# Hybrid decoder trunk, MLP stage: four additional matmuls behind the norm's mean, weights and operand from one tile, into a bank pair of the down products

## The chip, the core and the metric

One core of one Trainium2 chip runs the whole program. The metric is the time of one execution in device microseconds, as the median of several runs. Lower is better.

## The reference, cut to what matters

Four layers run one after the other over 512 tokens of width 1024: a latent attention mixer, an MLP, a gated linear attention mixer and a second MLP. All of it is in float32. The change touches both MLPs.

```
def rms_norm(x, gain):
    y = x * lax.rsqrt(jnp.mean(x * x, axis=-1, keepdims=True) + EPS)
    return y * gain

def sq_relu_mlp(xn, w_up, w_down):          # w_up 1024 x 4096, w_down 4096 x 1024
    hid = jnp.square(jax.nn.relu(xn @ w_up))
    return hid @ w_down
...
x = x + sq_relu_mlp(rms_norm(x, norm_mlp[i]), mlp_w_up[i], mlp_w_down[i])
return rms_norm(x, final_norm)
```

## The kernel before

**Precision.** A float32 matrix is held as two parts of type float32r, high and low (`split`, L110). The high part is a rounded copy written by ScalarE (ACT, L112), the low part is the remainder, written by VectorE (DVE, L115). A product is three matmuls on TensorE (PE): high by high, high by low, low by high. Each matmul instruction has a load of a 128x128 weight block of its own (a row of PEld) and a stream of the moving operand (a row of PE).

**The MLP.** Its two matrix products are written as block products with sums of blocks, so that fewer matmuls are needed. The up part works on 8 column blocks of `w_up` (`up_block`, L846), each with 7 products; the down part (`down_block`, L987) joins two of them and has 7 products too, woven between the up products. Each product runs through `matmuls` (L824), whose line L826 issues all of them: 128x128 weights and a moving operand of 256 columns. An up product is 24 of them, a down product 48. The weights are the split tiles `wh` and `wl` (three buffers each). The moving operands are the split input tiles `x0h` to `x7l`, their sums `T0h` to `T3l`, and for the down products the tile `h`. One product at the start of each MLP, that of block 1, takes its weights from a pair of tiles called `w`, which lie where `T3h` and `T3l` are put later (L907).

**Placement.** The author sets tile positions by hand with unused pieces (`PADS`, L91), and the first `h` tile of each down block begins 40 elements earlier in its buffer than the later ones (L1002 to L1004). In the built program, in bytes of a partition, `x0h` lies at 151136, the first `wh` at 34720, `w` at 214624, and the first `h` at 109248 with its `wh` at 42912.

**The place of the change.** `mlp` (L809) opens its banks (a pool with one bank for `seed`, three for `u`, two pairs for `d`). Its first two matmuls (L1163) have both weights and moving operand from `x0h` and write a `seed` bank; nothing reads that result. Then come the first products of blocks 0 and 1 (24 matmuls with `wh` and `wl`, 24 with `w`), and then the mean of the squares for the norm (L255 in `mean`, one float32 matmul of 512 columns that the trace shows as two rows). The products that follow need the mean only when their results are scaled (L890). Instruction order on an engine comes from a scheduling layer; `keep_in_program_order` (called `kept` here) holds single instructions where the code has them. Fifteen up products follow the mean before the first down product, whose banks (`d`, L1013) are free until then.

Of the kernel before, what the change touches and what calls it, by code (L numbers as in the profile page):

```python
# [10 lines left out]
F32 = mybir.dt.float32  # L11
# [7 lines left out]
P = 128  # L19
# [6 lines left out]
TH = S // 2  # L26
# [23 lines left out]
def trunk_kernel(ctx: ExitStack, tc: tile.TileContext, t_in: dict, out: bass.AP, out_row: bass.AP):  # L50
    nc = tc.nc
    PE, ACT, DVE, POOL, SP = nc.tensor, nc.scalar, nc.vector, nc.gpsimd, nc.sync
# [6 lines left out]
    def opened(name, side="left", space=None):  # L59
        es = ExitStack()  # L60
        kw = {"space": space} if space is not None else {"side": side}
        now[name] = es, es.enter_context(tc.tile_pool(name=uname(name), bufs=1, reuse_waits="tile", **kw))
        return now[name][1]
# [9 lines left out]
    def uname(s):  # L73
        count[0] += 1
        return f"{s}_{count[0]}"
# [34 lines left out]
    def split(src, hi, lo, hi_eng=ACT, lo_eng=DVE, order=lambda i: i):  # L110
        if hi_eng is ACT:
            raised.append(order(ACT.activation(hi, src, AF.Copy)))  # L112
        else:
            hi_eng.tensor_copy(hi, src)
        return lo_eng.tensor_tensor(lo, src, f(hi), ALU.subtract)  # L115
# [29 lines left out]
    def piece(raw, a, n, order=lambda i: i):  # L145
        hi = sb.tile([P, a, n], F32R, tag="wh", bufs=3, name=uname("wh"))
        lo = sb.tile([P, a, n], F32R, tag="wl", bufs=3, name=uname("wl"))
        cut_at.append(split(raw, hi, lo, order=order))
        return hi, lo
# [659 lines left out]
    def mlp(layer, nrm, nxt, final=False):  # L809
# [342 lines left out]
        mp = opened("mps", space=bass.MemoryType.PSUM)  # L1152
# [4 lines left out]
        for n, (m0, tk) in {2: (0, first), 3: (0, second), 4: (KH, first), 5: (KH, second)}.items():  # L1157
            acc[n] = xall[:, m0 : m0 + KH, tk]

        t = mp.tile([P, 512], F32, tag="seed", name=uname("ps"))  # L1160
        for h in range(2):
            x = quad["11"][0][0]
            PE.matmul(t[:, h * TH : (h + 1) * TH], x[:, :P], x, start=h == 0, stop=True, skip_group_check=True)  # L1163
        for b in range(2):
            wide[b] = halves(wide_raw())
        for b, t in enumerate(halves(wide_raw())):
            fills[b](t)
        kept = tc.keep_in_program_order
        for b in range(2):
            blocks[b].pop(0)()  # L1170
        t = nrm.combine(KH - 1, dp.tile([P, 4, TH], F32, tag="q", bufs=6, name=uname("q")))
        kept(nrm.mean())
        made[1]["21"] = piece(made[1]["a12"], KH, 256)
        kept(cut_at[-1])
        kept(nrm.combined(KH - 1, t))
# [466 lines left out]
    n_mix1 = Mixer(ND, inv_d, "mix", ND, "A")  # L1642
    n_mlp0 = mlp_norm(0)
    mlp0 = mlp(0, n_mlp0, n_mix1)
    out_proj(t_in["mla_w_o"][0], O, n_mlp0, mlp0, begun)
    next(mlp0, None)
# [5 lines left out]
    class Final:  # L1652
# [39 lines left out]
        def row(self, t, c, p):  # L1692
# [19 lines left out]
            for eng, q, cs in ((ACT, ACT, slice(0, 384)), (DVE, SP, slice(384, D))):  # L1712
# [4 lines left out]
                q.dma_start(o[:, cs], y[:, cs])  # L1717

    mlp1 = mlp(1, n_mlp1, Final(), True)
    out_proj(t_in["gla_w_o"][0], Y, n_mlp1, mlp1)  # L1720
    next(mlp1, None)
# [53 lines left out]
```

## Time and profile before

| | us |
|---|---|
| median of 3 runs | 1066.1 |
| lowest and highest of them | 1065.54, 1068.97 |
| the profiled execution's own time | 1065.53 |
| its span, first to last instruction | 1063.8 |
| PE busy in it | 1055.4 |
| PEld busy | 975.8 |
| DVE busy | 856.6 |
| ACT busy | 642.4 |

A start or a window is in microseconds from the start of the span. Matmuls overlap: a row of PE lasts longer than the distance to the next one, so the pace is read from the starts, or from the chain of waits, where each piece counts once and has its number of instructions.

### The profile page before, as it was taken

To read this page: it belongs to the slowest core of one execution; us is meant where nothing else is said; L and a number is where in the kernel's file an instruction comes from. 1 tells how busy PE (TensorE), PEld (TensorE's weight loads), DVE (VectorE), ACT (ScalarE), POOL (GpSimd) and SP (SyncE) were. 2 spreads that over 40 slices of the span, in tenths; PEclk is the share of its full clock that TensorE was granted. 3 is DMA by queue.
4 is the path that set the end of the run, shared out by engine and by line. 5 is a ranking of instruction groups with operands and counts; after the bars stand their busy time and mean duration, and the time that the engine had idled before them with its cause. 6 is when DMAs were issued, how large, how long until landed. Compare 5 with 4: busy or idle time off the path is not lost.

```text
span 1063.8 us, 17962 instructions
## 1 busy us (share of the span) xinstructions
PE 1055.4 (99%) x7332; PEld 975.8 (92%) x7332; DVE 856.6 (81%) x1186; ACT 642.4 (60%) x937; POOL 78.8 (7%) x104
## 2 busy tenths in 40 slices
PE   9999999999999999999999999999999999999997
PEld 7788988999999999988788888888999999999986
DVE  6789879899799789967565654678999799799965
ACT  6577645575667777644334734655665667776734
POOL 7400001000000000030000000001000000000000
PEclk9999999999999999999999999999999999999999
DMA  7312017765553663360222211238665555654412
GB/s 219 91 50 80 7 34 217 165 193 145 173 141 118 179 155 112 99 203 26 53 77 80 80 59 61 80 99 218 179 141 154 158 126 159 173 127 117 139 40 79
DMA packets 114946, 127.81 MB, mean 120 GB/s; under 512 B 8640, under 2 KB 86736, under 8 KB 114864
## 3 DMA queue, kind: packets, MB, share of 16 engines
q1 hardware_dynamic: 98832, 108.15, 32.0%
q0 software_dynamic: 13792, 16.80, 10.2%
q10 hardware_dynamic: 2240, 1.73, 0.5%
q8 instruction: 57, 0.93, 0.4%
q14 instruction: 25, 0.20, 0.1%
HBM read 124.56 MB, written 2.10 MB: 119 GB/s over the span
## 4 chain that ended last, share of the span: by engine, by line
PE 96%; DVE 2%; ACT 0%; DMA 0%; issue 0%; ACTq 0%; DVEq 0%
PE ps L826 51%; PE ps L120 13%; PE ps L122 13%; PE ps L121 13%; PE ps L1426 2%; PE ps L137 1%; PE ps L1465 0%; PE ps L1432 0%; PE ps L1412 0%; PE ps L685 0%; PE ps L686 0%; PE ps L684 0%; PE ps L682 0%; PE ps L683 0%; DVE stat L695 0%; DMA gains<-in_gains_dram 0%
## 5 line engine op out<-in xcount | busy, mean ns | idle before, releaser
L112 ACT ACTIVATE wh<-raw 128x1024 fp32r<-128x1024 f32 x208 | 219.8, 1060 | 152.7 <-PE ps L826 99.4
L115 DVE TENSOR_TENSOR wl<-raw,wh 128x1024 fp32r<-128x1024 f32 x208 | 251.8, 1220 | 25.4 <-ACT wh L112 25.1
L826 PE MATMUL ps<-h,wh 128*128 128x256 f32 x1344 | 168.6, 278 | 0.0
L826 PEld LDWEIGHTS ps<-h,wh 128*128 128x128 f32 x1344 | 161.2, 188 | 0.0
L120 PE MATMUL ps<-set,wh 128*128 128x512 f32 x232 | 91.3, 394 | 0.0
L826 PE MATMUL ps<-h,wl 128*128 128x256 f32 x672 | 91.2, 278 | 0.0
L121 PE MATMUL ps<-set,wh 128*128 128x512 f32 x232 | 90.7, 391 | 0.1
L122 PE MATMUL ps<-set,wl 128*128 128x512 f32 x232 | 90.7, 391 | 0.0
L112 ACT ACTIVATE wh<-wraw 128x1024 fp32r<-128x1024 f32 x41 | 43.1, 1057 | 74.2 <-PE ps L122 41.5
L826 PEld LDWEIGHTS ps<-h,wl 128*128 128x128 f32 x672 | 83.6, 188 | 0.0
L879 POOL DMA_DIRECT2D raw<-in_mlp_w_up_dram x20 | 25.8, 1290 | 707.4 <-DMA raw<-in_mlp_w_up_dram 330.5
L891 ACT ACTIVATE q<-q 128x512 f32<-128x512 f32 x64 | 40.3, 630 | 40.2 <-DVE q L890 39.8
L115 DVE TENSOR_TENSOR h<-q,h 128x1024 fp32r<-128x1024 f32 x44 | 53.7, 1222 | 9.1 <-ACT h L112 9.0
L120 PE MATMUL ps<-wh,set 128*128 128x512 f32 x144 | 59.7, 414 | 0.0
L115 DVE TENSOR_TENSOR wl<-wraw,wh 128x1024 fp32r<-128x1024 f32 x41 | 50.3, 1226 | 11.1 <-ACT wh L112 10.8
L122 PE MATMUL ps<-wh,set 128*128 128x512 f32 x144 | 56.3, 391 | 0.0
L121 PE MATMUL ps<-wl,set 128*128 128x512 f32 x144 | 56.2, 390 | 0.0
L121 PEld LDWEIGHTS ps<-set,wh 128*128 128x128 f32 x232 | 43.6, 188 | 9.9 <-DVE set L246 0.9
L122 PEld LDWEIGHTS ps<-set,wl 128*128 128x128 f32 x232 | 43.6, 188 | 9.4 <-DVE wl L115 0.5
L120 PEld LDWEIGHTS ps<-set,wh 128*128 128x128 f32 x232 | 43.5, 188 | 9.0 <-issue 0.2
L112 ACT ACTIVATE h<-q 128x1024 fp32r<-128x1024 f32 x44 | 46.0, 1049 | 0.2
L121 PE MATMUL ps<-hl,wh 128*128 128x512 f32 x96 | 37.4, 389 | 0.0
(512 smaller groups left out, 2789.4 us busy)
## 6 DMA issues: line engine op xcount, KB each, us to landing
raw<-in_mlp_w_down_dram SPq DMA_DIRECT2D x38, 1024.0 KB, 5.2
raw<-in_mlp_w_up_dram SPq DMA_DIRECT2D x70, 512.0 KB, 5.3
wraw<-in_gla_w_in_dram SPq DMA_DIRECT2D x11, 1024.0 KB, 5.1
raw<-in_mlp_w_up_dram POOLq DMA_DIRECT2D x20, 512.0 KB, 7.4
raw<-in_mlp_w_down_dram POOLq DMA_DIRECT2D x6, 1024.0 KB, 9.3
wraw<-in_mla_w_o_dram SPq DMA_DIRECT2D x8, 512.0 KB, 4.8
wraw<-in_gla_w_o_dram SPq DMA_DIRECT2D x8, 512.0 KB, 4.7
wraw_qn<-in_mla_w_uq_dram SPq DMA_DIRECT2D x6, 256.0 KB, 3.4
```

What stands on the lines that cost most here:

```text
L112: raised.append(order(ACT.activation(hi, src, AF.Copy)))
L115: return lo_eng.tensor_tensor(lo, src, f(hi), ALU.subtract)
L120: PE.matmul(psum, wh, xh, start=start, stop=False, **kw)
L121: PE.matmul(psum, wh, xl, start=False, stop=False, **kw)
L122: PE.matmul(psum, wl, xh, start=False, stop=stop, **kw)
L137: PE.transpose(psum, src, ident[: src.shape[0], : src.shape[0]])
L826: return PE.matmul(p[:, m * TH : (m + 1) * TH], w[i][:, k - k0, m * P : (m + 1) * P], x[k][j], start=start, stop=stop, skip_group_check=True,)
L879: POOL.dma_start(t, rows(half, trail), accum_op=ALU.add)
L891: ACT.activation(qs, qs, AF.Square)
L1426: PE.matmul(p[:, t * 64 : (t + 1) * 64].rearrange("p (n c) -> p n c", c=m), k[:, sl], later, start=True, stop=True)
```

## The change

The two matmuls at the head of the MLP become a function, called with 2 at the same place. After the mean it is called with 4: four matmuls of 128x128 weights and 256 moving columns, both from `x0h`, into a tile of the pair `d`. Each is held in program order. Nothing reads the result. Since the two buffers of `d` are taken in turn, each down product of the first block, and so on, now gets the other one of the pair.

```
-        t = mp.tile([P, 512], F32, tag="seed", name=uname("ps"))
-        for h in range(2):
+        def spare(t, n):
             x = quad["11"][0][0]
-            PE.matmul(t[:, h * TH : (h + 1) * TH], x[:, :P], x, start=h == 0, stop=True, skip_group_check=True)
+            for h in range(n):
+                i = PE.matmul(t[:, h * TH : (h + 1) * TH], x[:, :P], x, start=h % 2 == 0, stop=True, skip_group_check=True)
+                if n > 2:
+                    kept(i)
+
+        kept = tc.keep_in_program_order
+        spare(mp.tile([P, 512], F32, tag="seed", name=uname("ps")), 2)
...
         kept(nrm.mean())
+        spare(mp.tile([P, 4 * TH], F32, tag="d", bufs=2, name=uname("ps")), 4)
         made[1]["21"] = piece(made[1]["a12"], KH, 256)
```

On PE, in the first MLP, this is the difference around the mean (`acc` and `inv` are the mean's operands, `w` is the pair of block 1, `wh` the next product's weights):

```order
 L826 MATMUL ps_2303<-x3h_2226,w_2172 128x256 x2
 L255 MATMUL ps_2336<-acc_1947,inv_101 128x512
+L1163 MATMUL ps_2338<-x0h_1943 128x256 x4
 L826 MATMUL ps_2274<-x4h_1950,wh_2163 128x256
 L826 MATMUL ps_2274<-x4l_1951,wh_2163 128x256
```

Four rows are added; the second MLP has the same four at the same place, and no other row of PE moves. None of the four has a wait.

On ACT, a little later in the first MLP, these rows stand before the change (`q` is squared by L891 after DVE's L890 has scaled it; L938 copies the bank of block 1's third product, which its fourth product then goes on adding to):

```order
L112 ACTIVATE wh_2598<-raw_2169 128x1024
L891 ACTIVATE q_2273<-q_2273 128x512
L112 ACTIVATE wh_2628<-raw_2261 128x1024
L938 ACTIVATE mt_2564<-ps_2535 128x512
L891 ACTIVATE q_2273<-q_2273 128x512
L112 ACTIVATE wh_2670<-raw_2663 128x1024
L891 ACTIVATE q_2272<-q_2272 128x512
```

And these rows with it, where the numbers differ only because tiles are counted on:

```order
L112 ACTIVATE wh_2603<-raw_2169 128x1024
L891 ACTIVATE q_2273<-q_2273 128x512
L112 ACTIVATE wh_2633<-raw_2261 128x1024
L891 ACTIVATE q_2273<-q_2273 128x512
L938 ACTIVATE mt_2569<-ps_2540 128x512
L112 ACTIVATE wh_2675<-raw_2668 128x1024
L891 ACTIVATE q_2272<-q_2272 128x512
```

L938 and the second L891 have changed places, in both MLPs. Nothing moves on DVE, POOL or SP.

More of the change, by code (lines that the diff above doesn't have):

```diff
@@ L1167, in mlp @@
             fills[b](t)
-        kept = tc.keep_in_program_order
         for b in range(2):
```

## Prediction

> **What bounds the kernel now.** I read the page first, then PE's waits.
>
> ```profile
> PE 1055.4 (99%) x7332; PEld 975.8 (92%) x7332; DVE 856.6 (81%) x1186; ACT 642.4 (60%) x937; POOL 78.8 (7%) x104
> PEclk9999999999999999999999999999999999999999
> ```
> ```profile
> PE ps L1599 <- DVE ones L175: 1.2, 1, 1.2
> PE ps L685 <- ACT set L665: 0.3, 1, 0.3
> ```
>
> PE is busy 99% of the span at the full granted clock, and its whole list of waits is 1.5 us. So the time is the number of matmuls times the pace at which they follow each other; waits have nothing to give. The question is the pace. The chain of waits, taken stretch by stretch through both MLPs, gives it: start, length, line, count.
>
> ```profile
> 189.55 0.24 PE ps L1163 x2
> 195.40 0.86 PE ps L255 x2
> ...
> 189.79 2.50 PE ps L826 x22
> 192.29 2.87 PE ps L826 x24
> 196.25 42.05 PE ps L826 x357
> 238.54 5.37 PE ps L826 x46
> 244.25 81.74 PE ps L826 x694
> 332.18 59.27 PE ps L826 x523
> 397.40 64.95 PE ps L826 x573
> ...
> 743.29 42.05 PE ps L826 x357
> 791.29 81.62 PE ps L826 x693
> 879.11 59.28 PE ps L826 x523
> 944.57 64.72 PE ps L826 x571
> ```
>
> All of these are the same instruction, 128x128 weights and 256 columns, yet the pace has distinct values. From 196 to 326 us it is 42.05/357 = 117.8 ns and 81.74/694 = 117.8 ns. From 332 on it is 59.27/523 = 113.3 and 64.95/573 = 113.4 ns. The products with `w` run at 2.87/24 = 119.6 ns, the first product of a down block at 5.37/46 = 116.7 ns (below, the `h` product). The second MLP repeats this: 117.8, 117.8, 113.3, 113.3. I call 113.3 quick and 117.8 slow.
>
> The values sort by where the two operands lie, in the built program's placement. `wh` and `x0h` differ by 116416 bytes, 64 over a multiple of 128: this class runs slow or quick, for hundreds of matmuls without a change, whatever the product. `w` and `x0h` differ by 63488, a multiple of 128: about 120 ns. The first `h` and its `wh` differ by 66336, 32 over: 116.7 ns. So in the first class the pace is a state that is kept until something else comes in between. The slow state begins right behind the mean; it ends at the second `h` product, at 326; the third is at 391.
>
> **What sets the state.** These rows of PE show the two places where the kernel enters the first class: behind the two L1163 matmuls, and out of a stream of 512 columns in the GLA part.
>
> ```profile
> 189.39 0.40 PE L1163 MATMUL ps<-x0h 128*128 128x256 f32 x2
> 189.62 0.28 PE L826 MATMUL ps<-x0h,wh 128*128 128x256 f32 x1
> 189.75 0.28 PE L826 MATMUL ps<-x0l,wh 128*128 128x256 f32 x1
> ...
> 195.24 1.02 PE L255 MATMUL ps<-acc,inv 128*128 128x512 f32 x2
> 195.69 0.68 PE L826 MATMUL ps<-x4h,wh 128*128 128x256 f32 x1
> 196.21 0.28 PE L826 MATMUL ps<-x4l,wh 128*128 128x256 f32 x1
> ```
> ```profile
> 605.81 0.12 PE ps L120
> 608.99 0.12 PE ps L120
> ```
>
> Behind the two matmuls on one tile, the pace is quick after a few: from 189.79, 2.50/22 = 113.6 ns. Without them, out of the 512-column stream, 27 matmuls take 608.99 - 605.81 = 3.18 us, 117.8 ns each. Behind the mean it is slow too. A tile with itself has distance 0, the class of `w`. My reading, not shown: matmuls of this class bring weight load and moving stream into a fixed step, and from that step the first class falls into the quick state. Four behind the mean should do what two do at the head of the MLP.
>
> **The change, part by part.** The four added matmuls wait for nothing and nobody reads them. PE has no idle time to take them in, so all of their time is on the path: by `w`'s pace 4 x 0.12 = 0.48 us, by the quick pace 4 x 113.3 = 0.45 us, and by the first matmul behind L1163, which took 189.75 - 189.62 = 0.13 us, at most 0.52. I take 0.48 for each MLP.
>
> What they can give is the slow stretch: fifteen products of 24 from the mean to the first down product, then 29 of 24 up to the one at 326, 1056 matmuls. At 117.8 - 113.3 = 4.5 ns this is 4.70 us in each MLP. The two `h` products in between keep their pace: 116.7 when entered slow at 238, and when entered quick at 391, as this row shows with 5.49/47 = 116.8.
>
> ```profile
> 391.57 5.49 PE ps L826 x47
> ```
>
> That one entered quick and left quick (397.40), so I expect the state to outlive the `h` products at 238 and 326. Net 4.70 - 0.48 = 4.2 us in each MLP, 8.4 in all. The sum is made on the profiled execution: 1065.53 - 8.4 = 1057.1. That execution is 0.57 under the median of 1066.1, from which the same sum gives 1057.7. I say 1057.4.
>
> At one place a rule speaks against all this. The Trainium skill, "TensorE: Matmul & The Clock Gate", section "Step-by-step: what each phase is for", says that PE has two independent SBUF read ports, so that loading the next weights takes no read bandwidth from the running matmul. By it, the place of the operands could not matter and the sum would be 1065.53 + 0.96. The rows at 192.29 and 189.79 disagree: 119.6 and 113.6 ns for the same shape, with other tiles. The same page's section "Back-to-back issue gap" gives 262 cycles for 256 columns, by its 2.4 GHz an estimate of 109 ns; even the quick state here is slower.
>
> Whether the other engines keep up: the windows show DVE, ACT and PE in the slow stretch (busy us, count).
>
> ```profile
> 196.20:238.40 42.20, 42.20 (x361) 42.20 (x360) 38.87 (x42) 28.13 (x36) 1.28 (x1) 1.00 0.61 161
> 244.10:326.00 81.90, 81.90 (x698) 81.90 (x697) 74.40 (x68) 51.83 (x59) 3.85 (x3) 1.00 0.60 160
> 397.50:462.30 64.80, 64.80 (x574) 64.80 (x573) 61.76 (x59) 46.56 (x53) 6.36 (x9) 1.00 0.41 122
> ```
>
> DVE's 74.40 us must fit in 81.90 - 3.1 = 78.8 us: 94%. From 397 it already does 61.76 in 64.80, 95%, beside a quick PE without a wait. It fits, with little to spare.
>
> The swap on ACT has one price. In the second MLP L891 waits for DVE's L890, and L938 now stands behind it; PE's next product into the bank that L938 reads starts at 765.74.
>
> ```profile
> 763.37 0.68 DVE L890 SCALAR_TENSOR_TENSOR q<-q,rstd 128x512 f32<-128x512 f32 x1
> ```
> ```profile
> 763.24 0.58 ACT L938 ACTIVATE mt<-ps 128x512 f32<-128x512 f32 x1
> 764.09 0.64 ACT L891 ACTIVATE q<-q 128x512 f32<-128x512 f32 x1 [0.27 <-DVE q L890]
> ```
> ```profile
> 765.74 0.28 PE L826 MATMUL ps<-x4h,wh 128*128 128x256 f32 x1
> ```
>
> L938 would end at 764.09 + 0.64 + 0.58 = 765.3 at the latest. PE comes there after 8 of the 15 products, 192 matmuls: 765.74 + 0.48 - 0.86 = 765.36. So the cover is under 0.1 us. If it is gone, PE and the products queued behind wait some 0.1 us, worth nothing in itself; but a break could throw the state (the mean is one). In the first MLP the same cover is about half a us.
>
> **The rivals.** First, the state is lost at the `h` product of 238: for it speaks that such a product changed the state at 326; against it, the one at 391. Each MLP then gains 360 x 4.5 = 1.6 less 0.48, 2.2 in all: 1063.3.
>
> Second, the four do not kick: only 0.96 is added, 1066.5. For it: the state before them is that behind a mean, not that of a 512-column stream, and no row shows `w`'s class followed at once by the first. The rule of independent ports in the Trainium skill's page named above would give the same.
>
> Third, a part: one MLP loses the state early (the swap's break in the second: 4.2 + 0.4 gained, 1060.9), or no kick but the `h` product at 238 now ends quick (29 products, 3.1 less 0.48, twice: 1060.3).
>
> Fourth, slower: the four shift the step so that the `h` product at 326 no longer ends quick. Then the 523 matmuls from 332 on run slow until the one at 391: 2.3 + 0.48 us in each MLP, 5.6 in all, 1071.2. If 391 fails as well, the 573 behind it add 2.6 each, 1076. It decides at the first matmuls behind 331.6. For it: only one of two slow entries into an `h` product (326, not 238) ended quick, so the outcome hangs on the step.
>
> **How the numbers follow.** The forecast has 0.58, the first rival 0.08, the second 0.12, the third 0.14, the fourth 0.08. The lower end is the whole 4.70 twice with the four hidden, 1056.1. The forecast, third and first rival together are 0.80, so the upper end is the first rival's 1063.3, and by the median 1063.8. About 0.3%, 3.2 us, is what a measurement of this kernel can tell from no change: faster by more are the forecast and the third rival, 0.72; within are the first two rivals, 0.20; slower 0.08.
>
> **What would show it.** In the profile after: four L1163 rows behind L255, some 0.48 us on the chain, then from about 197 a pace of 113.3 instead of 117.8, and the next `h` product at about 237.4. The stretch from there to the third `h` product should also be at 113.3. A pace of 117.8 behind the four refutes the kick; 117.8 behind 238 alone is the first rival; 117.8 behind 331.6 the fourth. A wait of PE for ACT L938 near 765 would be the swap's.

## The result, and the profile after

The changed kernel takes 1057.97 us (median of 6 executions, 1056.94 to 1059.45), the kernel before, measured beside it, 1065.88 us (6 executions). The ratio is 0.9922, with a 95% interval from 0.9908 to 0.9936: 7.9 us less. The profiled execution took 1057.87 us, its span is 1056.1 us.

The page of the profile looks as before, with 8 matmuls more and PE busy 8 us less:

```profile
PE 1047.1 (99%) x7340; PEld 967.2 (92%) x7340; DVE 855.9 (81%) x1186; ACT 641.1 (61%) x937; POOL 78.4 (7%) x104
```

Taken for a whole MLP at once, the chain of waits puts everything behind the mean into one piece of 2304 matmuls, since nothing breaks it. Of the kernel before, in both MLPs:

```profile
196.25 266.33 PE ps L826 x2304
...
743.29 266.33 PE ps L826 x2304
```

And of the changed kernel, with the mean (L255) and the four added (L1163):

```profile
196.04 0.86 PE ps L255 x2
196.90 0.47 PE ps L1163 x4
197.38 261.68 PE ps L826 x2304
...
738.94 0.86 PE ps L255 x2
739.80 0.47 PE ps L1163 x4
740.27 261.68 PE ps L826 x2304
```

Each MLP loses 266.33 - 261.68 = 4.65 us and pays 0.47 for the four: 4.18, or 8.36 in both. Of that the two profiled executions show 1065.53 - 1057.87 = 7.66, because this one comes to its first MLP 0.64 us later (mean at 196.04, before at 195.40). That lies ahead of the first MLP, where the change touches nothing: in this execution PE waits 0.4 us for ScalarE (L245) and 0.3 us for VectorE (L246), waits that the profile of the kernel before doesn't have.

Taken stretch by stretch, the same chain gives the pace in the first MLP, from the mean to the end of the products:

```profile
197.49 40.48 PE ps L826 x357
238.19 5.37 PE ps L826 x46
243.91 80.65 PE ps L826 x711
328.88 58.82 PE ps L826 x519
393.99 64.94 PE ps L826 x573
```

40.48/357 and 80.65/711 are 113.4 ns, where it was 117.8; the first `h` product between them (238.19) still runs at 116.7 and now is entered quick and left quick. From 328 on the pace is what it was, 113.3.

VectorE keeps up: in the long quick stretch it is busy 74.91 of 80.10 us, 94% (the columns are the length, then the busy time of PE, PEld, DVE, ACT and POOL, PE's clock, the DMA share and GB/s), and PE waits for it nowhere in the MLPs.

```profile
243.90:324.00 80.10, 80.10 (x709) 80.10 (x708) 74.91 (x69) 52.04 (x59) 3.84 (x3) 1.00 0.62 164
```

The swap on ScalarE costs nothing either. These are its rows in the second MLP, and PE's first matmul into the bank that L938 reads:

```profile
760.60 0.64 ACT L891 ACTIVATE q<-q 128x512 f32<-128x512 f32 x1 [0.75 <-DVE q L890]
761.13 0.58 ACT L938 ACTIVATE mt<-ps 128x512 f32<-128x512 f32 x1
```
```profile
761.89 0.28 PE L826 MATMUL ps<-x4h,wh 128*128 128x256 f32 x1
```

L938 ends at 761.71, PE begins at 761.89, and its row is no longer than the others.

### The profile page after: what moved, and what is told of

Read it like the earlier page. It is cut to its first block, busy times and chain, and to the rows that moved or that the text cites. A ratio compares the mean times of both kernels' runs of the same rounds, so it can differ in the third digit from the quotient of the medians.

```text
span 1056.1 us, 17979 instructions
## 1 busy us (share of the span) xinstructions
PE 1047.1 (99%) x7340; PEld 967.2 (92%) x7340; DVE 855.9 (81%) x1186; ACT 641.1 (61%) x937; POOL 78.4 (7%) x104
## 4 chain that ended last, share of the span: by engine, by line
PE 98%; DMA 1%; DVE 1%; ACT 0%; issue 0%; ACTq 0%; DVEq 0%
PE ps L826 51%; PE ps L120 13%; PE ps L121 13%; PE ps L122 13%; PE ps L137 2%; PE ps L1431 2%; DMA xT<-in_x_dram 1%; PE ps L1470 0%; PE ps L685 0%; PE ps L686 0%; PE ps L684 0%; PE ps L683 0%; PE ps L682 0%; PE ps L1437 0%; PE ps L1417 0%; PE ps L255 0%
## 5 line engine op out<-in xcount | busy, mean ns | idle before, releaser
L115 DVE TENSOR_TENSOR wl<-raw,wh 128x1024 fp32r<-128x1024 f32 x208 | 251.5, 1219 | 19.8 <-ACT wh L112 19.4
L891 ACT ACTIVATE q<-q 128x512 f32<-128x512 f32 x64 | 40.3, 631 | 50.1 <-DVE q L890 50.1
L115 DVE TENSOR_TENSOR h<-q,h 128x1024 fp32r<-128x1024 f32 x44 | 53.7, 1221 | 8.8 <-ACT h L112 8.8
L115 DVE TENSOR_TENSOR wl<-wraw,wh 128x1024 fp32r<-128x1024 f32 x41 | 50.2, 1223 | 10.9 <-ACT wh L112 10.8
```

The lines of the kernel that those rows point to most:

```text
L891: ACT.activation(qs, qs, AF.Square)
```

## The experiments

The theory of the prediction: matmuls whose weights and moving operand lie a multiple of 128 bytes apart, standing last ahead of the products, set the quick pace. The rivals here: any four short matmuls do it, or the other bank of the pair `d`, or it takes one tile, or they may stand anywhere near. All kernels but one start from the changed kernel. In most of them `spare` got a third argument for the weights and a fourth that holds the matmuls in program order (the line of its matmul is then L1164). "Distance" is the number of bytes between weights and moving operand in a partition, modulo 128; "64 over" means 64 bytes over a multiple of 128. To kick means to set the quick pace behind the mean.

### Which matmuls, where, and how many

**Weights 64 bytes on in the same tile.**

```
-        spare(mp.tile([P, 4 * TH], F32, tag="d", bufs=2, name=uname("ps")), 4)
+        spare(mp.tile([P, 4 * TH], F32, tag="d", bufs=2, name=uname("ps")), 4, quad["11"][0][0][:, 16 : 16 + P], True)
```

> The four matmuls stay behind the mean, in the same bank and with the same operand, but their weights are taken 16 columns (64 bytes) further on in the tile. Theory (placement: matmuls whose weights and operand lie a multiple of 128 bytes apart set the quick state, those 64 bytes over don't): the four are of the same class as the x..h products, the slow pace of 117.8 ns stands behind the mean in both MLPs up to about 326 us and 873 us, and the four cost 4 x 0.118 = 0.47 us in each MLP, so 1065.9 + 0.94 = 1066.8 us. Rival (any four short matmuls behind the mean do, or the bank does it): 113.3 ns from the mean on, about 1058 us. From 1065 up speaks for the first, under 1060 for the second.

Measured: 1061.34 us, ratio 0.9959 [0.9945, 0.9974]. That is neither number. The chain shows why: the slow pace stands behind the mean as the theory said (42.28/359 = 117.8 ns), but the first `h` product, at 239.70, ends it, which in the kernel before only the second did (78.43/692 = 113.3 ns behind it).

```profile
197.07 0.47 PE ps L1164 x4
197.54 263.25 PE ps L826 x2304
...
197.54 42.28 PE ps L826 x359
239.70 5.61 PE ps L826 x48
245.66 78.43 PE ps L826 x692
```

So four matmuls of the wrong class don't set the pace, and yet their presence moves the end of the slow stretch from the second `h` product to the first, worth 266.33 - 263.25 = 3.08 us in each MLP.

**Weights from another tile, a multiple of 128 bytes away.**

```
-        spare(mp.tile([P, 4 * TH], F32, tag="d", bufs=2, name=uname("ps")), 4)
+        spare(mp.tile([P, 4 * TH], F32, tag="d", bufs=2, name=uname("ps")), 4, quad["11"][1][0][:, :P], True)
```

> The four matmuls stay behind the mean, with the weights from tile x1h and the operand from x0h: two tiles, 34816 bytes apart, a multiple of 128. Theory (placement): the step is set as by the change itself, 113.3 ns from the mean on in both MLPs, about 1058 us. Rival (it takes weights and operand from one tile, or the very same columns): 117.8 ns as before, 1065.9 + 0.94 = 1066.8 us.

Measured: 1057.43 us, 0.992 [0.9903, 0.9936], and the same piece of chain as with the change. One tile isn't needed; between this run and the one before, the distance is what differs.

```profile
196.91 261.68 PE ps L826 x2304
```

**The four ahead of the mean.**

```
+        spare(mp.tile([P, 4 * TH], F32, tag="d", bufs=2, name=uname("ps")), 4, None, True)
         kept(nrm.mean())
-        spare(mp.tile([P, 4 * TH], F32, tag="d", bufs=2, name=uname("ps")), 4)
```

> The same four matmuls ahead of the norm's mean instead of behind it, so that the two fp32 passes of the mean stand last before the products. Theory (what stands last before the x..h products sets their pace, and the mean sets the slow one): 117.8 ns behind the mean in both MLPs, about 1065.9 + 0.96 = 1066.8 us. Rival (the four set the quick state wherever they stand nearby, and it outlasts the mean): 113.3 ns, about 1058 us.

Measured: 1060.87 us, 0.9956 [0.9941, 0.9971]. Slow behind the mean (25.20/214 = 117.8), so the place does matter. But then something new: quick from 222.81 (10.33/91 = 113.5), slow again from 233.67 (4.95/42 = 117.9), and quick behind the first `h` product (78.09/689).

```profile
196.78 25.20 PE ps L826 x214
222.81 10.33 PE ps L826 x91
233.67 4.95 PE ps L826 x42
244.93 78.09 PE ps L826 x689
```

At both turns PE's rows have a short break, 0.24 us and 0.08 us by the starts. At the first, PE began just behind the end of ScalarE's L926, at 222.13 (its row, then PE's):

```profile
221.55 0.58 ACT L926 ACTIVATE ps<-mt 128x512 f32<-128x512 f32 x1
```
```profile
222.19 0.39 PE L826 MATMUL ps<-T0h,wh 128*128 128x256 f32 x1
222.41 0.28 PE L826 MATMUL ps<-T0l,wh 128*128 128x256 f32 x1
```

A short break can turn the pace, either way. It needn't: in the second MLP of this run a break of the same length, at 766.54, left the stream slow.

**One instead of four.**

```
-        spare(mp.tile([P, 4 * TH], F32, tag="d", bufs=2, name=uname("ps")), 4)
+        spare(mp.tile([P, 4 * TH], F32, tag="d", bufs=2, name=uname("ps")), 1, None, True)
```

> One such matmul behind the mean instead of four. If one is enough: 113.3 ns from the mean on, and 3 x 0.12 = 0.36 us less than the changed kernel in each MLP, 1058.0 - 0.7 = 1057.3 us. If the step takes several: 117.8 ns, 1065.9 + 0.24 = 1066.1 us. The theory leaves this open; the stretch of short matmuls behind the fp32 passes before the change (two of them ahead of the mean) doesn't decide it.

Measured: 1060.39 us, 0.9946 [0.9932, 0.9961], again neither number, and to the hundredth the piece of the first experiment. One matmul doesn't kick, and the pace is quick only behind the first `h` product.

```profile
197.81 263.25 PE ps L826 x2304
```

### What ends the slow pace: bank or count

Three experiments had landed at about 1061, where the slow pace ends at the first `h` product; the prediction had that as one half of its third rival, with 0.14 for both halves. Two things were moved in all three: the banks of the pair `d` (theory B) and the number of matmuls ahead of the `h` product (theory C). For C speaks a detail of the weight loads. In the slow stretch their rows come in threes, two of 187 or 188 ns and one of 192. Seen one load at a time, PEld of the kernel before has the long one right ahead of the first `h` product, which stays slow, and as the first load of the second one, which goes quick (line, tiles, count: shortest/median/longest ns, place):

```profile
L826 PEld LDWEIGHTS ps<-T3h,wl x1: 192/192/192, 238.3 to 238.3; 128*128 128x128 f32 x1
L826 PEld LDWEIGHTS ps<-h,wh x1: 192/192/192, 325.9 to 325.9; 128*128 128x128 f32 x1
```

With four matmuls more of the wrong class, the long load is the second one of the `h` product:

```profile
L826 PEld LDWEIGHTS ps<-h,wh x1: 188/188/188, 239.7 to 239.7; 128*128 128x128 f32 x1
L826 PEld LDWEIGHTS ps<-h,wh x1: 192/192/192, 239.8 to 239.8; 128*128 128x128 f32 x1
```

**Three matmuls 64 bytes over, in one tile of `d`.** B and C part here.

```
+        spare(mp.tile([P, 4 * TH], F32, tag="d", bufs=2, name=uname("ps")), 3, quad["11"][0][0][:, 16 : 16 + P], True)
```

> Three matmuls with weights 64 bytes over, in one bank of the down products; four such left the slow pace behind the mean standing, and yet the first h product at 240 us ended quick, which in the kernel before the one at 326 us did. Theory B: the products use the two down banks in turn, one more tile swaps them, and it is the bank of the first h product that decides; then quick from 245 us on as with four, 1061.3 - 2 x 0.12 = 1061.1 us. Theory C: the slow pace is a pattern of three matmuls (one weight load in three takes 192 ns, the others 187 or 188), and what decides is at which of the three the h product sets in: ahead of the two in the kernel before that stay slow it sets in right behind the long load, in all that go quick at another place. Three more leave that place as it was before: slow until the product at 326 us, about 1065.8 + 2 x 3 x 0.118 = 1066.5 us.

Measured: 1066.84 us, 1.0007 [0.9997, 1.0016]; C's 1066.5, not B's 1061.1. One matmul fewer in each MLP than in the first experiment, and 5.5 us more. The piece is the one of the kernel before, and the long load is back ahead of the `h` product:

```profile
196.72 266.33 PE ps L826 x2304
```
```profile
L826 PEld LDWEIGHTS ps<-T3h,wl x1: 192/192/192, 238.7 to 238.7; 128*128 128x128 f32 x1
```

**Four matmuls 64 bytes over, two in each of two tiles of `d`.**

```
+        for _ in range(2):
+            spare(mp.tile([P, 4 * TH], F32, tag="d", bufs=2, name=uname("ps")), 2, quad["11"][0][0][:, 16 : 16 + P], True)
```

> Four matmuls with weights 64 bytes over, two in each of two tiles of the down banks, so that the products use the banks as in the kernel before, while four more matmuls stand ahead of the h product. Theory B (bank): slow until the h product at 326 us, 1065.8 + 0.94 = 1066.8 us. Theory C (four is one more than three, so the place in the pattern moves): quick behind the first h product, as with four in one bank, 1061.3 us.

Measured: 1060.94 us, 0.9949 [0.9934, 0.9964]; C's 1061.3. The banks stand as before the change, and the first `h` product ends the slow pace all the same. B has fallen.

```profile
196.90 263.25 PE ps L826 x2304
...
741.34 264.35 PE ps L826 x2304
```

The second MLP of this execution took 1.10 us more, and that has another cause. At 981.86 PE's starts have a break of 0.2 us, just behind the end of VectorE's L115, which writes the low part of the weights. Up to there the pace was 113.3; behind it, it is 20.61/175 = 117.8 to the end of the MLP, for no `h` product of the odd distance follows.

```profile
980.59 1.21 DVE L115 TENSOR_TENSOR wl<-raw,wh 128x1024 fp32r<-128x1024 f32 x1
```
```profile
981.64 0.28 PE L826 MATMUL ps<-h,wh 128*128 128x256 f32 x1
981.86 0.50 PE L826 MATMUL ps<-h,wl 128*128 128x256 f32 x2
```
```profile
982.48 20.61 PE ps L826 x175
```

From the mean to the first `h` product there are 360 matmuls, a multiple of three. With none or three more it stays slow, with one or four it turns quick; two more, without a kick, were not run. In the traces of the kernel before and of the experiments a slow stretch runs into an `h` product of the odd distance 18 times; in the 4 that stay slow the long load is the last one ahead of it, in the 14 that turn quick it is the product's first or second. So what decides is the place in the pattern. The count sets that place only where nothing else moves it: in the second MLP of the third experiment no matmul was added behind the mean, but the break at 766.54 moved the pattern on, and the first `h` product ended quick.

**Two and three of the change's matmuls.** The call is that of the one, with 2 and with 3 as its number.

> Two matmuls of the change's kind behind the mean. One didn't set the quick step there, four do. If two do: 113.3 ns from the mean on, 1058.0 - 2 x 0.24 = 1057.5 us. If not: 117.8 ns behind the mean, and the first h product at about 238 us and 783 us ends quick whether it is the bank that decides there (theory B below) or the count (theory C), since both are moved: about 1060.6 us, as with one.

> Three of the change's matmuls behind the mean. If three set the quick step: 1058.0 - 2 x 0.12 = 1057.7 us. If not, the first h product tells theories B and C apart: with three more matmuls ahead of it the count stands where it stood in the kernel before, so by C the slow pace lasts to 327 us, 1065.9 + 0.72 = 1066.6 us, and by B (the other of the two down banks) it ends at 244 us, about 1060.9 us.

Measured: 1058.04 us with two (0.9922 [0.9907, 0.9937]), 1057.94 us with three (0.9922 [0.9907, 0.9936]). Both set the quick pace behind the mean; with three the count doesn't matter, since no `h` product is entered slow. But by their medians neither can be told from four. Of two, both MLPs:

```profile
196.55 261.66 PE ps L826 x2304
...
739.17 261.93 PE ps L826 x2304
```

In the second MLP 0.27 us come back, in two short waits. At 758.11, where the pace breaks by 0.14 us, PE began just behind the end of VectorE's L976 (757.29 + 0.68 = 757.97), and at 760.93 just behind that of L938.

```profile
757.29 0.68 DVE L976 TENSOR_TENSOR q<-ps,mt 128x512 f32<-128x512 f32 x1
```
```profile
758.11 0.36 PE L826 MATMUL ps<-T0h,wh 128*128 128x256 f32 x1
```

With three, only the second of them is left: L938 ends at 760.98 + 0.58 = 761.56, and the matmul into its bank, at 761.63, has a row of 0.37 us instead of 0.28; the next begins 0.21 us behind it instead of 0.11. That is the wait of the swap, which four just cover. In all these waits the pace stayed quick.

```profile
760.98 0.58 ACT L938 ACTIVATE mt<-ps 128x512 f32<-128x512 f32 x1
```
```profile
761.63 0.37 PE L826 MATMUL ps<-x4h,wh 128*128 128x256 f32 x1
761.84 0.28 PE L826 MATMUL ps<-x4l,wh 128*128 128x256 f32 x1
```

### The kick away from the mean, and the `h` products

**The four in the middle of the slow stretch.** They follow the fifth step of the loop over the blocks instead of the mean.

```
-        for b in (0, 0, 0, 0, 1, 0, 1, 1, 2, 1, 2, 1):
+        for i, b in enumerate((0, 0, 0, 0, 1, 0, 1, 1, 2, 1, 2, 1)):
...
+            if i == 4:
+                spare(mp.tile([P, 4 * TH], F32, tag="d", bufs=2, name=uname("ps")), 4, None, True)
```

> The four matmuls of the change not behind the mean but 168 products later, in the middle of the slow stretch. Theory (two or more matmuls with weights and operand a multiple of 128 bytes apart set the quick step wherever they stand): 168 of 1056 products at 117.8 ns, the rest quick: 1065.9 - 2 x (888 x 4.45 ns - 0.48 us) = 1059.0 us, and 113.3 ns from about 216 us and 763 us on. Rival (it takes the fp32 passes right ahead): slow to the h product at 239 us, which four more matmuls turn quick: about 1061.0 us.

Measured: 1060.98 us, 0.9952 [0.9939, 0.9964]. The rival is right: 21.79/185 = 117.8 ns behind the four. In the middle of a running slow stream they don't kick; directly behind the mean's two passes they do.

```profile
196.98 19.79 PE ps L826 x168
216.76 0.47 PE ps L1164 x4
...
217.24 21.79 PE ps L826 x185
```

**The `h` operands all at one distance.** First with the change, then without it.

```
-                    c = 0 if turn[1] != s else 40
+                    c = 40
```

> The changed kernel with one number of L1003 altered: the odd down operands always start 40 columns (160 bytes) into their tile, so that the first one of a down block lies 64 bytes over a multiple of 128 from its weights, as the others do, and no longer 32. Theory (place of weights and operand): the three h products of each MLP, 48 matmuls each, that run at 116.7 ns behind the change go to 113.3: 2 x 3 x 48 x 3.4 ns = 0.97 us, 1058.0 - 1.0 = 1057.0 us. Rival (these products are slow as the first of their block, whatever the address): 1058.0 us.

Measured: 1056.66 us, 0.991 [0.9897, 0.9922], by the medians 1.3 us under the changed kernel where 0.97 was forecast; the two intervals overlap, but the chain has the gain, 2 x (261.68 - 261.14) = 1.08. One piece, every matmul at 113.3 ns: 2304 x 113.33 = 261.1.

```profile
196.84 261.14 PE ps L826 x2304
```

> The kernel before, without the change, with the same edit of L1003. Theory: nothing but such an h product ends the slow pace, and none is left; it lasts from the mean to the end of the MLP's products at 462 us and 1009 us, so 525 + 573 matmuls more in each MLP at 117.8 instead of 113.3 ns and three times 48 at 117.8 instead of 116.7: 2 x (1098 x 4.44 + 144 x 1.1) ns = 10.1 us, 1065.9 + 10.1 = 1076.0 us. Rival (the slow pace ends of itself after some 1100 matmuls, or at the change of block): no more than the three products' saving, 1065.0 to 1065.9 us.

Measured: 1077.21 us, 1.0098 [1.0083, 1.0114]. The slow pace lasts to the end of each MLP, 2304 x 117.78 = 271.4:

```profile
200.04 271.36 PE ps L826 x2304
...
752.10 271.36 PE ps L826 x2304
```

The theory said 1076.0. The profiled execution, 1079.35, was the longest of the four and came to its first MLP 3.8 us later than the kernel before; inside the MLPs it is as forecast, 2 x (271.36 - 266.33) = 10.1.

So the `h` products with the odd distance cost 0.5 us in an MLP that is quick, and without them nothing ended the slow pace here in 2304 matmuls.

Distance, or each operand's own address? In the MLP the two can't be told apart, since in the built program almost every moving operand lies at 96 modulo 128 and every `wh` and `wl` at 32. The other parts of the kernel before speak for distance. The 27 matmuls from 605.81, which the prediction shows at 117.8 ns, have it the other way round, weights at 96 and operand at 32, so 64 over too. And four matmuls of the attention mixer with both at 32, distance 0, begin at 73.01, 73.13, 73.25 and 73.37, 120 ns apart like those with `w`, which have both at 96. For the kick itself it stays open: the matmuls that kick have their weights at 96, those that don't at 32.

**Two matmuls and one distance together.**

> Both together: two of the change's matmuls instead of four, and the odd operands always 40 columns in. From the parts: 1058.0 - 2 x 0.24 - 0.97 = 1056.5 us. If the saved matmuls vanish in other waits, as the time with two (1058.04 by its median, its profiled run's span 1055.3) leaves open: 1057.0 us.

Measured: twelve executions, in two groups: six from 1055.94 to 1057.79 us, six from 1065.02 to 1066.42 us; their median of 1061.4 is the time of neither. The profiled one is of the first group. It has the two short waits in the second MLP (261.38 against 261.12), and came out of both quick:

```profile
196.70 261.12 PE ps L826 x2304
...
738.77 261.38 PE ps L826 x2304
```

The groups are some 9 us apart, about 2000 matmuls by 4.45 ns. My reading, not shown, since no execution of the second group was profiled: there one of these waits turns the pace, as the break at 981.86 did above, and no `h` product of the odd distance is left to mend it. Behind the second wait, at 760.7, 2112 matmuls of the MLP are left, an estimate of 9.4 us.

## Why the prediction was right, point by point

- **Pace by count.** Right. 4.65 us per MLP where 4.70 was forecast, 0.47 for the four where 0.48 was; the time 1057.97 where 1057.4 was.
- **The quick pace outlives the `h` products.** Right, in both MLPs; the first rival is out.
- **VectorE keeps up.** Right: 94%, no wait. There is little to spare, as forecast: with two matmuls PE stands for VectorE's L976 once, 0.14 us.
- **The swap's cover.** Thin but enough: 761.71 against 761.89. With three or two matmuls it isn't, and in the second MLP the saved time comes back in waits.
- **What sets the pace.** The reading was half right. Which matmuls kick follows the class by distance: 64 bytes over failed with three and with four, a multiple of 128 did it from one tile and from two. But it isn't so that such matmuls set the step wherever they stand, and one is too few: shown are two, three and four directly behind the mean. The prediction took its recipe from the head of the MLP, where the two stand behind another stream; that head was never run without them, and no row spoke for the place behind the mean, as the second rival says. That it would do there, and with four, was in part luck.
- **The rival without a kick** was priced wrongly. It assumed that all else would stay, 1066.5. Four without a kick give 1061.3, because four is one more than a multiple of three and the first `h` product then ends the slow pace; this was the second half of the third rival, which gave 1060.3, so all the chance of a failed kick belonged there. So 4.5 of the 7.9 us (by the chain 2 x (3.08 - 0.47) = 5.2 of 8.36) would have come from the count alone, and the kick, which the forecast rested on, brought only the rest. 1061.3 lies in the forecast's range too, so the time alone doesn't show the kick; the pace behind the four does.
- **The rival that is slower** named the right dependence (the step at which an `h` product is entered) and a price of the right size: with nothing to end the slow pace the MLPs take 271.36 us each, 1077.2, where it gave 1076 for the changed kernel. The change doesn't enter an `h` product slow, so it never came up.
- **The rule of independent read ports** (the Trainium skill, "TensorE: Matmul & The Clock Gate", section "Step-by-step: what each phase is for"): by it, as the prediction read it, the place of the operands could not matter. For these matmuls it does: moving only the `h` operand by 160 bytes took an MLP from 261.68 to 261.14 us, and without the change from 266.33 to 271.36. Whether it is the load of weights that takes something from the running matmul, no run here shows.

What stays open: what in PE makes the two paces, why one matmul is not enough behind the mean, why the four fail in a running stream, and which break turns the pace. In the profiled executions PE has ten short breaks behind the mean; three turned the pace (222.19 and 233.39 of the third experiment, 981.86 of the four in two tiles), seven left it, and their length doesn't sort them: 0.08, 0.2 and 0.24 us turned it, 0.07 to 0.14 and 0.24 us did not.

## What to carry to other kernels

Where one engine is busy 99% and the same instruction shows two paces, divide each piece of its chain by its count before looking for waits: 4% of pace over a thousand matmuls outweighed every wait in this trace. Before a matmul is added or taken away ahead of such a stretch, ask what its count does to the step at which the next different product is entered, and test it with a dummy of another class, which separates the count from the effect that is meant. The version with the lowest time here (1056.66 us) has also lost the `h` products that mend a lost pace; a version like it with two matmuls was 9 us slower in half its executions.

## What the runs showed of the hardware that was not expected

- The pace of a stream of 128x128 by 256-column matmuls has two values that hold for a whole MLP: 2304 of them took 261.14 or 271.36 us, with the granted clock at 0.997 or more in both.
- The slow one is a pattern of three (weight loads of 188, 188 and 192 ns), and the time depended on the place in that pattern at which another product set in: one dummy matmul fewer in each MLP, 5.5 us more.
- Breaks of PE of 0.24 and 0.08 us turned the pace in both directions within 11 us, and one of 0.2 us turned it in another run; seven others of 0.07 to 0.24 us did not.
